# Scan decays by spread float32r products with an added mask, and a replanned attention, in a hybrid SSD / attention / PEER layer on one Trainium2 core

## The chip, the cores and the metric

The kernel runs on one core of one Trainium2 chip, in one launch. The metric is the device time of an execution in microseconds (us); it holds the span that the profile shows, from the first to the last instruction, and a little around it. The engines are PE (matrix products), DVE (vector), ACT (scalar functions), POOL and SP. SP, ACT and POOL also issue transfers (DMA). Each engine takes its instructions in program order, and an instruction that waits holds up what stands behind it on its engine.

## The reference

One layer (DEPTH = 1) on 512 latent and 256 context tokens of width 1024: a norm, one projection, three parallel mixers (a bidirectional Mamba-2 scan, pooling, neighbourhood attention), one output projection with a gated residual, a second norm, and a PEER feed-forward with 16384 experts. The scan is where the change is largest. Per chunk of 128 tokens, head and direction it computes

```
a_cs   = jnp.cumsum(a, axis=-1)                      # a = dt * a_head, per token and head
lmat   = jnp.exp(segsum(a))                          # exp(cs[l] - cs[s]) for s <= l, else 0
cb     = jnp.einsum('bclhn,bcshn->bhcls', cc, bc)    # one 128x128 matrix per chunk and group of 8 heads
y_diag = jnp.einsum('bhcls,bcshp->bclhp', cb * lmat, xd)   # xd = x * dt
y_off  = jnp.einsum('bclhn,bchpn->bclhp', cc, states[:, :-1]) * in_decay
```

once forward and once on the flipped sequence; the two results are added, gated by silu(z) and normed.

## The kernel before

The program runs through stages that the profile shows one behind the other: input projection and convolution (to about 203 us), the decays of the scan and the projection of V for the context (to 220), the scan (220 to 389), attention (to 486), the output projection and second norm (to about 560), and the PEER stage, which fills the rest of the span. Each projection product is written as three float32r products (high x high, low x high, high x low) with helper lines L186 to L188; a weight block arrives as `wraw`, ACT writes its float32r part `wh` (L176) and DVE (or POOL) the remainder `wl` (L179).

**The scan.** Its work is laid on steps by hand: `at(step, f, ...)` puts a piece on a step, and `run(step)` issues the pieces, each step together with six products of the projections of z, V and q. There are 16 *units* (4 chunks x 4 units of 4 heads), one every two steps, apart from two steps at the change of a chunk. A unit (c, u) consists of

- `u_in`: DVE writes `ms0` and `ms1` (mask times a, 128x512 each), and ACT writes eight 128x128 tiles, cb masked by a triangle and scaled by dt, into `t1` (forward) and `t2` (backward)
- `u_mm`, a step later: two float32 products of 128x512 that sum both directions' log decays into one PSUM tile `mm`
- `u_exp`, a step later: ACT takes one Exp over 128x512 into `ee`, DVE adds `t1` and `t2`
- `u_mul`, a step later: DVE multiplies by `ee`
- `u_diag`, a step later: PE's four products `yd` (float32, 128x64) with x.

Per chunk there are `c_mm` (cb of both groups, into an `mm` tile) and `c_mask` (four DVE products with a triangle). `st_in`, `st_mm`, `st_add` carry the states (`xd`, `mm<-xd,Bn`, `sfw` and `SB`), `o_mm`/`o_add` the part from the states. All of `u_mm`, `c_mm`, `st_mm`, `o_mm` share two PSUM buffers `mm`; `psT` (tile `pt`) has one buffer, `psY` holds `yd`. `f_load` to `f_store` gate, norm and transpose the result.

**Around it.** `decays` (L703) makes six Exps from sums of `an` (= a) by constant triangles. `q_out` scales q out of PSUM into `qT`. In the attention, `items` lists the weight blocks and mixer results that are split, and `OI` the steps at which that is issued; `o_first` starts the output projection with the pool part (`mBh`, `mBl`), and `o_part` goes on with it between the attention's own products (`sps`, `pt`, `po`). After it, `h_square` and `norm2` make the second norm of four token tiles, `norm2_split` its float32r parts `u2h` and `u2l`, and `q_part` and the first `u_block`s are the first products that use them.

## Time and profile before

| what | value |
| --- | --- |
| median of 3 runs | 1778.91 us (1778.72 to 1785.7) |
| profiled execution, its own time | 1779.43 us |
| its span, first to last instruction | 1777.6 us |
| TensorE clock granted, mean | 0.999 |
| PE busy | 1750.7 us (98%) |
| DVE, ACT, POOL busy | 1396.9, 837.6, 354.3 us |

The profile's page gives busy times by engine, the chain of work that ended last, and the costliest groups of instructions. Its trace can be asked for stretches of time, for groups by line and shape, for what an engine waited on, and for single instructions. In such rows L with a number is the line of the kernel before, a tile's buffer number is left out, and `<-ACT ee L895` behind an idle time names the instruction whose end released it. Matmul records overlap, since the engine is pipelined, so the distance from start to start is what a product takes in a row of products.

### The profile page before, as it was taken

The page shows a single profiled execution, that of the slowest core. Times are in us where ns is not written, and L with a number is a line of the kernel's source. Part 1 is how long each engine was busy: PE and PEld are TensorE (multiplying, and loading weights), DVE is VectorE, ACT ScalarE, POOL GpSimd, SP SyncE. Part 2 cuts the span into 40 slices and gives each one's busy share as a digit, 9 for nine tenths or more (in the row PEclk, how much of TensorE's full clock was granted, in tenths as well). Part 3 has the DMA queues.
Part 4 walks back from the last instruction along what each step waited for, and adds up shares of the span by engine and source line. Part 5 has one row for each costly group of instructions (what it writes and reads, how often), then busy time and mean ns, then how long its engine had stood idle before and what let it go on. Part 6 is the DMA issues. An engine that isn't in the chain of part 4 may idle for free.

```text
span 1777.6 us, 26116 instructions
## 1 busy us (share of the span) xinstructions
PE 1750.7 (98%) x9583; PEld 1503.8 (85%) x9583; DVE 1396.9 (79%) x2648; ACT 837.6 (47%) x1495; POOL 354.3 (20%) x248
## 2 busy tenths in 40 slices
PE   7999999999999999999999999999999999999998
PEld 6888776677788889999999998888888888888886
DVE  5689477976536589889999978878878888888876
...
GB/s 361 124 154 226 166 83 67 70 241 234 96 135 160 126 116 112 187 252 253 335 354 333 345 315 399 403 353 342 360 341 352 328 401 365 346 348 342 367 251 82
DMA packets 191905, 454.38 MB, mean 256 GB/s; under 512 B 13817, under 2 KB 117497, under 8 KB 173825
## 3 DMA queue, kind: packets, MB, share of 16 engines
...
q14 instruction: 54, 0.43, 0.1%
HBM read 400.09 MB, written 54.67 MB: 256 GB/s over the span
## 4 chain that ended last, share of the span: by engine, by line
PE 91%; DMA 3%; DVE 3%; ACT 2%; issue 1%; SPq 0%; POOL 0%; ACTq 0%; DVEq 0%; POOLq 0%
PE pv L188 10%; PE pv L186 10%; PE pv L187 10%; PE pu L186 9%; PE pu L188 9%; PE pu L187 9%; PE acc L186 5%; PE acc L188 5%; PE acc L187 5%; PE mm L889 2%; PE acc L406 1%; PE acc L411 1%; PE acc L408 1%; PE gdps L1695 1%; PE gdps L1696 1%; PE sps L1091 1%
## 5 line engine op out<-in xcount | busy, mean ns | idle before, releaser
L179 DVE TENSOR_TENSOR wl<-wraw,wh 128x1024 fp32r<-128x1024 f32 x294 | 367.3, 1262 | 101.5 <-ACT wh L176 99.1
L176 ACT ACTIVATE wh<-wraw 128x1024 fp32r<-128x1024 f32 x328 | 341.0, 1052 | 206.1 <-PE acc L187 76.7
L186 PE MATMUL pu<-u2h,wh 128*128 128x384 f32 x1024 | 349.7, 342 | 0.0
L188 PE MATMUL pu<-u2h,wl 128*128 128x384 f32 x1024 | 345.5, 337 | 0.4 <-DVE wl L179 0.4
L187 PE MATMUL pu<-u2l,wh 128*128 128x384 f32 x1024 | 344.8, 337 | 0.8 <-DVE u2l L179 0.8
L1634 POOL DMA_INDIRECT row<-in_peer_uv,idxG x128 | 156.6, 1223 | 807.9 <-DVE accG L1648 713.9
L186 PE MATMUL pv<-wh,wwh 128*128 128x512 f32 x768 | 301.2, 392 | 0.6 <-ACT wh L176 0.6
L187 PE MATMUL pv<-wl,wwh 128*128 128x512 f32 x768 | 300.5, 391 | 0.8 <-DVE wl L179 0.8
L188 PE MATMUL pv<-wh,wwl 128*128 128x512 f32 x768 | 300.9, 392 | 0.0
L187 PEld LDWEIGHTS pu<-u2l,wh 128*128 128x128 f32 x1024 | 192.5, 188 | 2.9 <-DVE u2l L179 1.1
L186 PEld LDWEIGHTS pu<-u2h,wh 128*128 128x128 f32 x1024 | 192.3, 188 | 1.8
L188 PEld LDWEIGHTS pu<-u2h,wl 128*128 128x128 f32 x1024 | 192.2, 188 | 1.3 <-DVE wl L179 1.3
L188 PEld LDWEIGHTS pv<-wh,wwl 128*128 128x128 f32 x768 | 144.2, 188 | 32.2
L187 PEld LDWEIGHTS pv<-wl,wwh 128*128 128x128 f32 x768 | 144.2, 188 | 31.9 <-DVE wl L179 1.8
L186 PEld LDWEIGHTS pv<-wh,wwh 128*128 128x128 f32 x768 | 144.2, 188 | 30.7 <-ACT wh L176 1.0
L1648 DVE SCALAR_TENSOR_TENSOR accG<-row,wG,accG 128x1024 f32<-128x1024 f32 x127 | 162.5, 1279 | 4.6 <-ACT wG L1643 3.3
L1639 DVE CUSTOM_DVE_ANT_0 row<-row,u2G 128x1024 f32<-128x1024 f32 x128 | 155.2, 1219 | 0.0
L176 ACT ACTIVATE wwh<-acl 128x384 fp32r<-128x384 f32 x86 | 45.2, 526 | 205.7 <-DVE acl L1807 139.7
L1698 ACT ACTIVATE stg<-gdps 128x512 f32<-128x512 f32 x96 | 101.4, 1169 | 19.4 <-PE gdps L1696 12.9
L179 POOL TENSOR_TENSOR wl<-wraw,wh 128x1024 fp32r<-128x1024 f32 x34 | 81.7, 2406 | 108.4 <-ACT wh L176 76.9
L1801 ACT ACTIVATE act<-pu 128x384 f32<-128x384 f32 x42 | 20.6, 491 | 159.3 <-PE pu L188 159.3
L1807 DVE TENSOR_TENSOR act<-act,gd 128x384 f32<-128x384 f32 x42 | 23.4, 558 | 84.4 <-ACT act L1801 84.4
...
## 6 DMA issues: line engine op xcount, KB each, us to landing
wraw<-in_peer_ut SPq DMA_DIRECT2D x128, 512.0 KB, 8.4
wraw<-in_peer_uv SPq DMA_DIRECT2D x128, 512.0 KB, 9.1
...
```

Source lines behind the costliest of these rows:

```text
L176: S.activation(hi, full, AF.Copy)
L179: (eng or V).tensor_tensor(lo, full, hi.bitcast(F32), ALU.subtract)
L186: PE.matmul(ps, ah, bh, start=start, stop=False)
L187: PE.matmul(ps, ah, bl, start=False, stop=False)
L188: PE.matmul(ps, al, bh, start=False, stop=stop)
L889: PE.matmul(ps, m, ms[d].rearrange("p a b -> p (a b)"), start=d == 0, stop=d == 1)
L1634: G.indirect_dma_start(out=rows[k], out_offset=None, in_=A["peer_uv"], in_offset=bass.IndirectOffsetOnAxis(ap=idxG[:, k:k + 1], axis=0))
L1639: V.tensor_tensor_reduce(row[:, 0:D], row[:, 0:D], u2G, 1.0, 0.0, ALU.mult, ALU.add, actG[:, k:k + 1])
L1648: V.scalar_tensor_tensor(accG, row[:, D:2 * D], wG[:, k:k + 1], accG, ALU.mult, ALU.add)
L1698: S.activation(stg[:, :, t0:t0 + 4].rearrange("p a t -> p t a"), ps, AF.Copy, scale=1.0 / GSCALE)
L1801: S.activation(ac[a], pu[:, :TD], AF.Gelu)
L1807: V.tensor_tensor(xq, xq, gds.pop(a), ALU.mult)
```

## The change

1. **Log decays.** Behind the pool projection PE makes the cumulative sums of `a` for all chunks and heads in both directions (`pcs`, 64 rows x 256). They are split into a float32r part and its remainder (`csT[0]` by ACT, `csT[1]` by DVE), written to DRAM (`cs_d`) and read back as 16 rows of a tile `rows` (128 x 2048) whose other 112 rows POOL sets to zero. `u_mm` becomes four float32r products: a column of `sel` spread over 128 columns picks the two rows (part and remainder) of a chunk and direction and puts their sum on all partitions; `idr` (identity) adds `neg0` or `neg1`, which hold -1e30 in the triangle that is to vanish. The forward direction goes into `pt` (psT), the backward one into `mm`.
2. **Exps.** `u_in` is gone. `u_exp` takes eight Exps of 128x128 with the negative cumulative sum (`ncs`) as bias per partition, and ACT scales two of the four backward tiles by dt; `u_mul` scales the other two on DVE (128x256), joins the directions with four `scalar_tensor_tensor` of 128x128, and multiplies by `cb`, which `c_copy` now only copies from PSUM. `u_diag` and `y_add` come a step later. The tiles of z that sat in `ms0`/`ms1` move into `SB`.
3. **Attention.** The last `q_out` is on DVE, `qT` is two tiles, block w0 is split earlier and w6 is split within the attention, the low part of pool block 4 is made by DVE rather than POOL, and its eight products stand at steps +5 and +6 rather than +2. The loads of `h` go from steps 12 to 15 to 36 to 45, that of `g1r` from 16 to 34.
4. **Second norm.** The mean square is put together by one DVE operation ahead of the square root rather than two around it; the norm of the third tile comes ahead of a split; the first q products and the first two PEER blocks take their late operand's products last (`mm_late`); the split of the first PEER block's low part goes from POOL to DVE.

```diff
+    ncs = [si.tile([P, NX, NH], F32, name=f"ncs{d}") for d in range(2)]
+    csT = [ad1.tile([NX * NH, 2, P], F32R, name=f"csT{i}") for i in range(2)]
+    pcs = psG.tile([P, 512], F32, name="acc")[0:NX * NH, 0:2 * P].rearrange("p (d t) -> p d t", d=2)
+    for d, m in enumerate((U_in, L_in)):
+        tc.keep_in_program_order(PE.matmul(pcs[:, d, :], an[:, d, 0:NX, :].rearrange("p t h -> p (t h)"), m, start=True, stop=True))
+    S.activation(csT[0], pcs, AF.Copy)
+    V.tensor_tensor(csT[1], pcs, csT[0].bitcast(F32), ALU.subtract)
+    for i in range(2):
+        nc.scalar.dma_start(cs_d[i].rearrange("d p t -> p d t"), csT[i].bitcast(F32))
     decays([(SU, 0, enF), (SL, 1, enB), (ONE, 0, toF)])
...
+        if b == 3:
+            V.tensor_scalar(dst, acc, HD ** -0.5, None, ALU.mult)
+        else:
+            S.activation(dst, acc, AF.Copy, scale=HD ** -0.5)
...
+    rows = m1.tile([P, NH * P], F32R, name="rows")
+    G.memset(rows[0:112].bitcast(F32), 0.0)
+    nc.scalar.dma_start(rows[112:P].bitcast(F32), cs_d.rearrange("i d (c h) t -> (i d c) (h t)", c=NX))
+    sel = m1.tile([P, 8], F32R, name="sel")
+    V.tensor_tensor(sel, ident[:, 112:120], ident[:, 120:P], ALU.add)
+    idr = m1.tile([P, P], F32R, name="idr")
+    V.tensor_copy(idr, ident)
+    negs = []
+    for d, m in enumerate((SU, SL)):
+        negs.append(m1.tile([P, P], F32R, name=f"neg{d}"))
+        V.tensor_scalar(negs[d], m, -1e30, None, ALU.mult)
...
-            V.tensor_tensor(ms[d], mb(msk), hb(an[:, d, c, hs]), ALU.mult)
...
-        for d, (t, tri) in enumerate(((t1, "U"), (t2, "L"))):
-            for j in range(4):
-                S.activation(t[:, j, :], cbm[g, tri], AF.Copy, scale=dtn[:, d, c, u * 4 + j:u * 4 + j + 1])
...
+    def u_mm(c, u):
+        un[c, u] = []
+        for d in range(2):
+            ps = psM.tile([P, 512], F32, name="mm") if d else psT.tile([P, 4, P], F32, name="pt").rearrange("p a b -> p (a b)")
+            x = 4 * d + c
+            PE.matmul(ps, sel[:, x:x + 1].broadcast_to([P, P]), rows[:, u * 512:(u + 1) * 512], start=True, stop=False)
+            PE.matmul(ps, idr, mb(negs[d]), start=False, stop=True)
+            un[c, u].append(ps)
+
+    def u_exp(c, u):
+        pf, pb = un[c, u]
         t1 = m2.tile([P, 4, P], F32, name="t1", bufs=3)
         t2 = m2.tile([P, 4, P], F32, name="t2")
...
-        S.activation(ee.rearrange("p a b -> p (a b)"), ps, AF.Exp)
-        V.tensor_tensor(t1, t1, t2, ALU.add)
-        un[c, u] = [ee, t1]
+        for j in range(4):
+            h = u * 4 + j
+            S.activation(t1[:, j, :], pf[:, j * P:(j + 1) * P], AF.Exp, bias=ncs[0][:, c, h:h + 1])
+        for j in range(4):
+            h = u * 4 + j
+            S.activation(t2[:, j, :], pb[:, j * P:(j + 1) * P], AF.Exp, bias=ncs[1][:, c, h:h + 1])
+        for j in range(2):
+            S.activation(t2[:, j, :], t2[:, j, :], AF.Copy, scale=dtn[:, 1, c, u * 4 + j:u * 4 + j + 1])
...
-        V.tensor_tensor(t1, t1, ee, ALU.mult)
+        t1, t2 = un[c, u]
+        V.tensor_tensor(t2[:, 2:4, :], t2[:, 2:4, :], dtn[:, 1, c, u * 4 + 2:u * 4 + 4].unsqueeze(2).broadcast_to([P, 2, P]), ALU.mult)
+        for j in (2, 3, 0, 1):
+            V.scalar_tensor_tensor(t1[:, j, :], t1[:, j, :], dtn[:, 0, c, u * 4 + j:u * 4 + j + 1], t2[:, j, :], ALU.mult, ALU.add)
+        V.tensor_tensor(t1, t1, mb(cbm[u // 2, "r"]), ALU.mult)
...
-            at(b + 2 * u + 4, u_diag, c, u)
-            at(b + 2 * u, u_in, c, u)
+            at(b + 2 * u + 5, u_diag, c, u)
             at(b + 2 * u + 1, u_mm, c, u)
...
-    items = [("w", 4), ("p", 4), ("p", 5), ("w", 5), ("s", 0), ("s", 1), ("s", 2), ("s", 3), ("w", 0), ("w", 1), ("w", 2), ("w", 3)]
+    items = [("w", 4), ("p", 4), ("p", 5), ("w", 5), ("s", 0), ("w", 0), ("s", 1), ("s", 2), ("s", 3), ("w", 1), ("w", 2), ("w", 3), ("w", 6)]
...
-    OI = [0, 0, 3, 4, 8, 10, 13, 15, 16, 28, 41, 54]
+    OI = [0, 0, 3, 4, 8, 11, 14, 18, 21, 28, 41, 54, 58]
...
-    at(O0 + 2, o_first, True)
+    at(O0 + 5, o_first, True, (0, 1))
+    at(O0 + 6, o_first, True, (2, 3))
...
-        at(O0 + 12 + t, nc.scalar.dma_start, h[:, t, :], A["x"][t * P:(t + 1) * P, :])
+        at(O0 + 36 + 3 * t, nc.scalar.dma_start, h[:, t, :], A["x"][t * P:(t + 1) * P, :])
...
+    def mm_late(ps, us, c, w, ks, late, first, last):
+        n = len(ks)
+        terms = [(k, x) for k in ks for x in ([(0, 0), (1, 0)] if late == "w" else [(0, 0), (0, 1)])]
+        terms += [(k, (0, 1) if late == "w" else (1, 0)) for k in ks]
+        for i, (k, (a, b)) in enumerate(terms):
+            PE.matmul(ps, w[b][:, k, :], us[a][:, k, c], start=first and i == 0, stop=last and i == 3 * n - 1)
...
-    q_part(0, early, range(4))
+    mm_late(pqs[0][:, early], (u2h, u2l), early, wqs[0], range(4), "u", True, False)
...
-    e_split(AHEAD[0], 0, G)
+    e_split(AHEAD[0], 0, None, alows)
```

On PE, at the second unit of chunk 0, the order before (names are output <- moving or stationary operands; `acc` rows belong to the z projection):

```order
1013 L889 MATMUL mm<-ms_2133,cst 128x512
1014 L889 MATMUL mm<-ms_2135,cst 128x512
1015 L186 MATMUL acc<-wh,uh 128x512
1016 L187 MATMUL acc<-wl,uh 128x512
1017 L188 MATMUL acc<-wh,ul 128x512
1018 L186 MATMUL acc<-wh,uh 128x512
1019 L187 MATMUL acc<-wl,uh 128x512
1020 L188 MATMUL acc<-wh,ul 128x512
1021 L831 MATMUL mm<-xd,Bn 128x512
1022 L909 MATMUL yd<-xsn,t_2097 128x64 x4
```

and with the change, from the state's product behind the first unit to the end of the second unit:

```order
1025 L859 MATMUL mm<-xd,Bn 128x512
1026 L186 MATMUL acc<-wh,uh 128x512
1027 L187 MATMUL acc<-wl,uh 128x512
1028 L188 MATMUL acc<-wh,ul 128x512
1029 L186 MATMUL acc<-wh,uh 128x512
1030 L187 MATMUL acc<-wl,uh 128x512
1031 L188 MATMUL acc<-wh,ul 128x512
1032 L934 MATMUL yd<-xsn,t_2139 128x64 x4
1033 L902 MATMUL pt<-rows,sel 128x512
1034 L903 MATMUL pt<-neg_2041,idr 128x512
1035 L902 MATMUL mm<-rows,sel 128x512
1036 L903 MATMUL mm<-neg_2043,idr 128x512
```

Two float32 products have become four float32r ones; between two units there are still twelve `acc` products and one `mm<-xd`, and `yd` has moved from behind `mm<-xd` to a place directly ahead of the next unit's first product.

On ACT, the second and third unit of chunk 0 before:

```order
159 L895 ACTIVATE ee<-mm 128x512
160 L882 ACTIVATE t_2187<-cbU_2077,dtn 128x128 x4
161 L882 ACTIVATE t_2188<-cbL_2079,dtn 128x128 x4
162 L895 ACTIVATE ee<-mm 128x512
163 L882 ACTIVATE t_2230<-cbU_2077,dtn 128x128 x4
```

and the first two of the change:

```order
158 L912 ACTIVATE t_2139<-pt,ncs_1888 128x128 x4
159 L915 ACTIVATE t_2140<-mm,ncs_1889 128x128 x4
160 L917 ACTIVATE t_2140<-t_2140,dtn 128x128 x2
161 L176 ACTIVATE wh<-wraw 128x1024
162 L912 ACTIVATE t_2187<-pt,ncs_1888 128x128 x4
163 L915 ACTIVATE t_2188<-mm,ncs_1889 128x128 x4
164 L917 ACTIVATE t_2188<-t_2188,dtn 128x128 x2
```

The eight small operations were independent of `u_mm`; now they all come behind it and read its PSUM tiles, and two more follow. On DVE, by the diff, four operations of 128x512 in a unit have become one of 128x256, four of 128x128 and one of 128x512, all behind the Exps, and four of 128x128 per chunk have become one copy of 128x256.

On PE at the second pair of heads of the attention, where the low products of the pool part (`mBl`) stand, before:

```order
1449 L1225 MATMUL acc<-wl,mBh 128x512
1450 L1222 MATMUL acc<-wh,mBl 128x512 x8
1451 L1091 MATMUL sps<-kT,qT 128x256 x4
1452 L1121 MATMUL pt<-cst,pr 128x128 x8
1453 L186 MATMUL acc<-wh,mBh 128x512
```

and with the change:

```order
1481 L1250 MATMUL acc<-wl,mBh 128x512
1482 L1116 MATMUL sps<-kT,qT_95 128x256 x4
1483 L1146 MATMUL pt<-cst,pr 128x128 x4
1484 L1247 MATMUL acc<-wh,mBl 128x512 x4
1485 L1146 MATMUL pt<-cst,pr 128x128 x4
1486 L1247 MATMUL acc<-wh,mBl 128x512 x4
1487 L186 MATMUL acc<-wh,mBh 128x512
```

The eight products that stood ahead of the scores `sps` now stand four by four behind the two transposes `pt`, which share the one buffer of `pt`.

## Rows read from the trace of the kernel before

**Rows 1.** The profile's page: busy time and share of the span by engine, and the chain that ended last by engine.

```profile
PE 1750.7 (98%) x9583; PEld 1503.8 (85%) x9583; DVE 1396.9 (79%) x2648; ACT 837.6 (47%) x1495; POOL 354.3 (20%) x248
PE 91%; DMA 3%; DVE 3%; ACT 2%; issue 1%; SPq 0%; POOL 0%; ACTq 0%; DVEq 0%; POOLq 0%
```

**Rows 2.** Busy time of each engine in stretches of the span: length, then PE, PEld (weight loads), DVE, ACT, POOL with their instructions, granted clock, DMA share and GB/s.

```profile
250.00:300.00 50.00, 50.00 (x210) 34.77 (x208) 37.79 (x62) 24.82 (x65) 1.01 (x1) 1.00 0.24 69
300.00:348.00 48.00, 47.31 (x188) 31.19 (x188) 44.53 (x58) 23.33 (x62) 15.38 (x9) 1.00 0.20 61
389.00:486.00 97.00, 93.85 (x652) 67.49 (x654) 58.80 (x172) 57.98 (x127) 27.47 (x17) 1.00 0.54 177
```

**Rows 3.** The chain of waits from 203 to 389 us: start, length, what. The first is the decays' sums, then the first and the last of the 16 units' products.

```profile
207.09 1.31 PE acc L701 x12
232.41 1.72 PE mm L889 x4
346.09 1.72 PE mm L889 x4
```

**Rows 4.** PE's instructions in order of time around two units of the scan: start, time of the record, line, operation.

```profile
267.93 1.88 PE L889 MATMUL mm<-ms,cst 128*128 128x512 f32 x4
...
270.10 0.39 PE L188 MATMUL acc<-wh,ul 128*128 128x512 f32 x1
270.33 0.39 PE L186 MATMUL acc<-wh,uh 128*128 128x512 f32 x1
...
274.15 1.88 PE L889 MATMUL mm<-ms,cst 128*128 128x512 f32 x4
```

**Rows 5.** DVE's groups by line and shape from 220 to 389 us: busy time of the group, mean of one in ns, idle time before.

```profile
L877 DVE TENSOR_TENSOR ms<-cst,an 128x512 f32<-128x512 f32 x32 | 22.3, 737 | 0.0
L901 DVE TENSOR_TENSOR t<-t,ee 128x512 f32<-128x512 f32 x16 | 15.3, 957 | 0.0
L896 DVE TENSOR_TENSOR t<-t,t 128x512 f32<-128x512 f32 x16 | 13.1, 817 | 0.0
L869 DVE TENSOR_TENSOR cbU<-mm,cst 128x128 f32<-128x128 f32 x8 | 2.3, 284 | 1.0 <-PE mm L861 0.9
```

**Rows 6.** DVE's groups by line and shape over the whole span: operations of the shapes that the change adds, from other stages.

```profile
L179 DVE TENSOR_TENSOR ucl<-uf,uch 128x256 fp32r<-128x256 f32 x8 | 3.3, 418 | 0.0
L1342 DVE TENSOR_SCALAR uf<-pt,sc2T,sh2T 128x128 f32<-128x128 f32 x16 | 5.5, 405 | 3.3 <-PE pt L1332 3.2
L1591 DVE SCALAR_TENSOR_TENSOR j<-pf,a4i 128x128 f16<-128x128 f32 x4 | 1.1, 288 | 0.0
```

**Rows 7.** ACT's groups by line and shape from 203 to 389 us.

```profile
L882 ACT ACTIVATE t<-cbU,dtn 128x128 f32<-128x128 f32 x64 | 20.3, 391 | 4.5 <-DVE cbU L869 4.5
L895 ACT ACTIVATE ee<-mm 128x512 f32<-128x512 f32 x16 | 9.6, 598 | 47.5 <-PE mm L889 39.2 <-DVE t L901 5.9 <-DVE t L896 2.4
L703 ACT ACTIVATE inB<-acc 128x96 f32<-128x96 f32 x1 | 0.3, 295 | 0.0
```

**Rows 8.** ACT and its queue in order of time behind the pool projection.

```profile
207.85 0.33 ACTq L679 DMA_DIRECT2D mix_d<-pa  x1
...
211.22 1.06 ACT L176 ACTIVATE wh<-wraw 128x1024 fp32r<-128x1024 f32 x1 [0.76 <-PE acc L188]
```

**Rows 9.** DVE in order of time at the start of the scan, and PE's first state product, which uses the last of these.

```profile
220.09 0.16 DVE L535 SCALAR_TENSOR_TENSOR sc2T<-pt,colv 128x8 f32<-128x8 f32 x1
220.47 2.00 DVE L179 TENSOR_TENSOR wl<-wraw,wh 128x1024 fp32r<-128x1024 f32 x1 [0.22 <-ACT wh L176]
222.39 2.39 DVE L824 TENSOR_TENSOR xd<-xsn,enB 128x512 f32<-128x512 f32 x1
...
225.96 1.02 PE L831 MATMUL mm<-xd,Bn 128*128 128x512 f32 x2
```

**Rows 10.** PE's waits in order of time: the wait for an Exp in the scan, then those in the attention and the second norm; the time in brackets is how long PE stood idle.

```profile
314.20 1.12 PE L831 MATMUL mm<-xd,Bn 128*128 128x512 f32 x2 [0.69 <-ACT ee L895]
...
389.20 0.70 PE L1091 MATMUL sps<-kT,qT 64*128 64x256 f32 x4 [0.69 <-ACT qT L769]
...
398.56 0.63 PE L1121 MATMUL pt<-cst,pr 128*128 128x128 f32 x4 [0.78 <-ACT pT L1126]
...
416.38 0.63 PE L1121 MATMUL pt<-cst,pr 128*128 128x128 f32 x4 [1.05 <-ACT pT L1126]
...
452.14 1.13 PE L1091 MATMUL sps<-kT,qT 64*128 64x256 f32 x6 [0.75 <-ACT pr L1108]
...
543.77 0.36 PE L187 MATMUL acc<-u2l,wh 128*128 128x256 f32 x1 [0.43 <-DVE ssq L1322]
...
551.52 0.44 PE L187 MATMUL pu<-u2l,wh 128*128 128x384 f32 x1 [0.84 <-DVE u2l L179]
```

**Rows 11.** ACT, its queue and DVE in order of time at three of those waits: the copy of `pT` behind a transfer's issue, the last `qT` with the `wl` that DVE has at the time, and the pair of `u2l`.

```profile
415.20 0.33 ACTq L1032 DMA_DIRECT2D nb<-in_nabias  x1
415.63 0.60 ACT L1126 ACTIVATE pT<-pt 128x512 f32<-128x512 f32 x1 [1.12 <-PE po L1139]
...
388.55 0.60 ACT L769 ACTIVATE qT<-acc 128x512 f32<-128x512 f32 x1 [2.90 <-PE acc L188]
...
387.76 1.22 DVE L179 TENSOR_TENSOR wl<-wraw,wh 128x1024 fp32r<-128x1024 f32 x1
...
548.73 3.34 DVE L179 TENSOR_TENSOR u2l<-uf,u2h 128x512 fp32r<-128x512 f32 x2
```

More of the change, by code (lines that the diff above doesn't have):

```diff
@@ L269, in build @@
     kT = na1.tile([P, 4, NTOK], F32, name="kT")
-    qT = na1.tile([P, 4, SEQ], F32, name="qT")
+    qTs = [na1.tile([P, 2, SEQ], F32, name=f"qT{i}") for i in range(2)]
     vc = na1.tile([P, 2, 512], F32, name="vc")
@@ L305, in build @@
     xT = a1.tile([P, KB, NTOK], F32, name="xT")
-    kf, qf, vf = (ap.rearrange("p a b -> p (a b)") for ap in (kT, qT, vc))
-    xin = [kf[:, t * D:(t + 1) * D] for t in range(3)] + [qf[:, t * D:(t + 1) * D] for t in range(2)] + [vf]
+    kf, q0f, q1f, vf = (ap.rearrange("p a b -> p (a b)") for ap in (kT, *qTs, vc))
+    xin = [kf[:, t * D:(t + 1) * D] for t in range(3)] + [q0f, q1f, vf]
     for t in range(NT):
@@ L878, in u_in @@
+    def u_exp(c, u):
+        pf, pb = un[c, u]
         t1 = m2.tile([P, 4, P], F32, name="t1", bufs=3)
         t2 = m2.tile([P, 4, P], F32, name="t2")
-        for d, (t, tri) in enumerate(((t1, "U"), (t2, "L"))):
-            for j in range(4):
-                S.activation(t[:, j, :], cbm[g, tri], AF.Copy, scale=dtn[:, d, c, u * 4 + j:u * 4 + j + 1])
-        un[c, u] = [ms, t1, t2]
-    def u_mm(c, u):
-        ms, t1, t2 = un[c, u]
-        ps = psM.tile([P, 512], F32, name="mm")
-        for d, m in enumerate((SU, SL)):
-            PE.matmul(ps, m, ms[d].rearrange("p a b -> p (a b)"), start=d == 0, stop=d == 1)
-        un[c, u] = [ps, t1, t2]
@@ L1204, in build, with o_first @@
     O0 = A0
-    OI = [0, 0, 3, 4, 8, 10, 13, 15, 16, 28, 41, 54]
+    OI = [0, 0, 3, 4, 8, 11, 14, 18, 21, 28, 41, 54, 58]
     at(O0, i_load, 3)
     at(O0, i_load, 4)
-    before(O0, i_low, 1)
     before(O0, i_high, 1)
-    for i in range(2, 12):
+    at(O0 + 2, i_low, 1)
+    for i in range(2, len(items)):
         before(O0 + OI[i], i_high, i)
         at(O0 + OI[i], i_low, i)
-    at(O0 + 16, row_bc, g1r, 1, 0, nc.scalar)
-    def o_first(low):
-        for t in range(NX):
+    at(O0 + 34, row_bc, g1r, 1, 0, nc.scalar)
+    def o_first(low, ts):
+        for t in ts:
             ts_ = slice(t * P, (t + 1) * P)
@@ L1228, in o_part @@
         out_mm(accs[t], ispls[kk], kk, t, False, False)
[L1229 to L1230 removed]
+    at(O0 + 1, o_first, False, range(NX))
+    at(O0 + 5, o_first, True, (0, 1))
+    at(O0 + 6, o_first, True, (2, 3))
     for j, kk in enumerate((5, 0, 1, 2, 3)):
@@ L1278, in out_end @@
         S.activation(tmp, h[:, t, hs], AF.Square, accum_out=ssq[:, t, half:half + 1])
+        V.scalar_tensor_tensor(ssq[:, t, 0:1], ssq[:, t, 0:1], 1.0 / D, epsc, ALU.mult, ALU.add)
     for kk in (6, 7):
-        w = out_w(kk, 0)
+        w = ispls[6] if kk == 6 else out_w(kk, 0)
         for t in range(NX):
@@ L1428, in build @@
     ahead = ahead_steps(lambda: u_depth[0])
-    pus = [u_block(*sp[AHEAD[0], 0])]
-    norm2_T(3)
-    norm2_scale(3)
-    pus.append(u_block(*sp[AHEAD[1], 0]))
+    pus = []
+    for m in range(2):
+        pus.append(psu())
+        mm_late(pus[m][:, :TD], (u2h, u2l), slice(0, TD), sp[AHEAD[m], 0], range(KB), "w", True, True)
+        if m == 0:
+            norm2_T(3)
+            norm2_scale(3)
     norm2_split(3, 0)
```

65 lines of the change are left out of this document (34 added, 31 removed).

## The prediction, made before the change was run

> **What bounds the kernel now.** I read the page first, for the engine on which the chain lies: PE is busy 98% of the span and carries 91% of the chain, DVE and ACT 3% and 2% [rows 1]. Then the stretches, for what each stage waits on: from 250 to 300 us PE is busy all 50.00, from 300 to 348 it is 47.31 of 48.00 while DVE is busy 44.53 (93%) and ACT 23.33, and in the attention PE has 3.15 us idle of 97 [rows 2]. So inside the scan the price of an edit is the PE time that it takes away, as long as DVE and ACT keep up; in the attention it is the single waits of PE. The chain of waits gives the size of the scan's part: `u_mm` stands in it with 1.72 us for each of 16 units [rows 3]. The clock is at its upper level throughout (1.00 in each stretch of [rows 2]), so nothing is to be had from it.
>
> **Scan, PE.** Six projection products follow each other every 0.23 us (270.10, 270.33 in [rows 4]); they are float32r and 128x512, as the four new ones are. `u_mm` was two float32 products, four records, 1.72 us. Four times 0.23 is 0.92, so a unit saves 0.80 and the 16 units 12.8 us. That is the largest term, and PE is what the chain follows there, so I take it whole. The period of two steps was 274.15 − 267.93 = 6.22 us [rows 4] and becomes 5.42. The bounds: no PE time saved if a product with a spread operand takes 0.43 (half a float32 product, two records of 0.43 each), and 12.8 at the rate of the row. No row has a product whose stationary or moving operand is one column or one block spread by repetition; the nearest in type and size is that of [rows 4], and I take it.
>
> **Added PE work.** The cumulative sums are two float32 products of 64x128 outputs, four records; the decays' twelve records of 96 columns took 1.31 us [rows 3], so four take some 0.45.
>
> **Front of the scan.** ACT gets a copy of 64x256 and two transfer issues of 0.33 each [rows 8], with the wait for DVE's remainder between, some 1.5 us in all, ahead of the Exps of the decays; behind those the first `wh` waited 0.76 for PE [rows 8]. So 0 to 0.8 us can reach PE. DVE gets four small operations (`sel`, `idr`, `neg0`, `neg1`) behind `sc2T`; at 0.28 (cbU, [rows 5]) they take 1.1 us, of which 0.22 was idle time ahead of `wl`, and push `xd`, which ended at 224.78 and is used at 225.96 [rows 9]: 1.18 us of slack against 0.9, so nothing or a few tenths. `rows` is issued behind three `wh`, some 12 us ahead of the first `u_mm` at 232.41 [rows 3]; POOL's zeroing lies there too. I take +0.5 for the front, bounds 0 and 1.6.
>
> **Scan, DVE and ACT.** DVE's unit was two `ms` (22.3/32 each), the sum (13.1/16), the product (15.3/16), and a quarter of four triangle products of 0.28 [rows 5]: 1.39 + 0.82 + 0.96 + 0.28 = 3.45 us. It becomes 0.42 for 128x256 and four times 0.29 for 128x128 [rows 6], 0.70 for 128x512 (22.3/32, [rows 5]), 0.1 for the copy: 2.4. With the dearer 0.405 [rows 6], an operation with two operands per partition, it is 2.8. In 300 to 348 there are six units; DVE goes from 44.5 to some 38.3 us, while the stretch itself shrinks by 4.8 to 43.2: 89% rather than 93%. It is no looser by much, but no tighter. ACT's unit was eight small ones at 20.3/64 = 0.32 and one Exp of 0.60 [rows 7]: 3.1 us; ten small ones are 3.2 at the same price. Exps of 128x96 out of PSUM took 0.295 [rows 7], so 0.32 is a fair price for 128x128, and 0.39 (the mean of one, unoverlapped) the upper bound: 3.9. ACT then has 3.2 to 3.9 of a period of 5.42, with `wh` (1.06, [rows 8]) in about every other one.
>
> What is new is the wait. Before, ACT's small ones needed no `u_mm`; now all eight Exps stand between `u_mm` and the release of its two PSUM buffers. `pt` and the `mm` of the unit are wanted again a period later, 4.5 us after `u_mm` ends; eight Exps take 2.5 to 3.1. That holds in the steady part. Where `c_mm` or an `o_mm` or state product comes between, the buffer is wanted after one `xd` product (0.86, half of 1.72) and six of 0.23: 2.2 us. At some six such places PE could wait 0.3 to 0.9 us: 0 to 4, I take +1.2. At one of them it waited before, 0.69 for the single `ee` [rows 10], and that wait is replaced: −0.7. Net +0.5. `u_diag` comes one step later to make room for the longer ACT and DVE chain, 3.2 + 2.4 us and what queues there, of some 9 us from `u_mm` to `yd`; it needs no more.
>
> At this place a rule speaks against the change. The Trainium skill ("VectorE: DVE Perf Modes", section "The TRN2 errata — SBUF-src ops pay a fixed extra latency per instruction") has vector and scalar operations pay a fixed cost per instruction and advises tiles of at least 512 elements. Its table would give an Exp of 128 columns out of PSUM 300 cycles at 1.2 GHz, an estimate of 0.25 us, against 0.57 for one of 512, so eight cost 2.0 where one cost 0.57. The trace agrees that small ones are dear (0.32 for 128 columns, 0.60 for 512, [rows 7]); but the kernel before pays for eight of them already. What it would make of the time is the first rival.
>
> **Attention and tail.** `q_out` of the last block goes to DVE, which is then in a `wl` from 387.76 to 388.98 [rows 11]; its 128x512 (0.70, as `ms` in [rows 5]) would end at about 389.7 where ACT's ended at 389.15. PE waits for it (0.69 at 389.20, [rows 10]); that grows by 0.5, bounds 0 and 0.9. The wait of 0.78 at 398.56 is the second `pt` for the copy of the first out of the one buffer; four products of 0.23 now stand between and cover it. The wait of 1.05 at 416.38 is a `pT` that ACT began at 415.63, held by the issue of `nb` at 415.20 [rows 11] behind loads of `h`, which now come 24 steps later: gone too. The wait of 0.75 at 452.14 stays, its two weight splits stand together as before. Together −1.8; bounds −3 (all 3.15 idle us of [rows 2]) and +2, should a moved split come late. In the second norm PE waits 0.43 for a `u2l` and 0.84 for the next [rows 10]; late operands last covers the first with eight products, and the second is shortened since the pair of `u2l` took 3.34 us [rows 11] in place of two times 0.7 beside POOL's split, which is moved to DVE behind them: −1.0, bounds −1.3 and +1.
>
> **Sum.** −12.8 + 0.45 + 0.5 + 0.5 + 0.5 − 1.8 − 1.0 = −13.65. The profiled execution took 1779.43, its span 1777.6 and 1.83 around it; 1779.43 − 13.65 = 1765.8. The median of the runs, 1778.91, lies 0.5 lower, so I forecast 1765.3. The PEER stage is untouched and only starts earlier. A measurement of this kernel can hardly tell less than 0.5%, 8.9 us, from no change.
>
> **Rivals.** (1) ACT becomes the gate, by the rule above. If a small Exp costs 0.39 and does not overlap, ten are 3.9, and with `wh` or a z copy every period is full; a unit then loses some 0.5 us to `pt` or `mm`, 8 us in all: 1773, within 0.5%. For it: the Exps are in order behind `wh`, which itself waits for PE. Against: ACT is busy half the time from 250 to 348 [rows 2], and 20.3/64 is with overlap. 0.12. (2) The spread products don't run at the float32r rate. At the float32 price of 0.86 each, `u_mm` takes 3.44 us, 1.72 more, 27.5 us over 16 units: 1779 + 27.5 − 1 = 1805. It decides from 0.43 per product on, where nothing is saved. No row speaks for it. 0.04. (3) The replanned attention goes wrong: the splits moved to DVE there make `mBl` or `qT` late at several places, 3 to 6 us more than forecast: 1768 to 1771, on either side of the 1770.0 from which it counts as faster. 0.10. (4) The waits cost nothing and the attention loses all its idle time: −12.8 + 0.45 − 0.7 − 3 − 1.3, 1762. 0.12.
>
> **Chances.** The forecast with its own bounds, 1762 to 1769, has 0.62. Faster by over 0.5% holds the forecast, (4), and a good half of (3): 0.80. Within 0.5% holds (1) and the rest of (3): 0.16. Slower: (2), 0.04. The range goes from 1759.5, a little beyond (4) since its bounds add up, to 1772.5, past (3) and just short of (1), and leaves out about 0.16.
>
> **What would show it.** `u_mm` should stand as four records 0.23 apart, and two units 5.4 us apart; PE should be busy as fully as before from 250 to 348, with DVE just under 90%. PE waits on ACT's `t` ahead of `c_mm` or `mm<-xd` would be the new wait; if they stand at every unit, rival 1 is right. The scan should end about 12 us earlier, and the first `sps` of the attention wait about a microsecond for DVE. The forecast is wrong if a new product's start to start is well over 0.23, or if DVE runs solid.

## The result, and the profile after

The changed kernel takes 1767.76 us (median of 6 runs, 1765.78 to 1770.83) against 1779.93 us of the kernel before (median of 6); the ratio is 0.9937, 95% interval 0.9926 to 0.9947, so 9 to 13 us faster. A second set of runs gave 1767.12 against 1778.91, ratio 0.9936 (0.9919 to 0.9953). The forecast was 1765.3 with 1759.5 to 1772.5. The profiled execution took 1769.83 us, its span is 1768.1.

The page after, busy time and chain, which answer to [rows 1]:

```profile
PE 1740.0 (98%) x9587; PEld 1505.5 (85%) x9587; DVE 1388.4 (79%) x2678; ACT 835.1 (47%) x1511; POOL 348.6 (20%) x247
PE 93%; DVE 4%; ACT 1%; DMA 1%; issue 1%; ACTq 0%; POOL 0%; DVEq 0%; SPq 0%
```

PE lost 10.7 us of work and is still the chain. The stretches, as in [rows 2] (the second and third moved by the time already won):

```profile
250.00:300.00 50.00, 50.00 (x234) 38.56 (x233) 41.25 (x81) 30.38 (x92) 0.00 (x0) 1.00 0.30 90
300.00:345.00 45.00, 44.11 (x191) 31.39 (x190) 40.86 (x69) 22.49 (x63) 17.69 (x11) 1.00 0.25 74
378.00:475.00 97.00, 94.32 (x664) 68.08 (x664) 61.89 (x177) 57.99 (x126) 25.82 (x16) 1.00 0.58 178
```

PE is about as full in the scan as before (44.11 of 45.00, 47.31 of 48.00 before), and DVE is 91% busy from 300 to 345 (40.86 of 45.00). Two units of the scan on PE, the answer to [rows 4]:

```profile
270.45 0.48 PE L902 MATMUL pt<-rows,sel 128*128 128x512 f32 x1
270.77 0.40 PE L903 MATMUL pt<-neg,idr 128*128 128x512 f32 x1
271.00 0.40 PE L902 MATMUL mm<-rows,sel 128*128 128x512 f32 x1
271.24 0.40 PE L903 MATMUL mm<-neg,idr 128*128 128x512 f32 x1
...
275.90 0.48 PE L902 MATMUL pt<-rows,sel 128*128 128x512 f32 x1
```

The spread products start 0.23 us apart, as the projections do, and the period is 5.45 us. Only the first of a unit, now directly behind `yd`, takes 0.32.

To see where time went I compare the start of the same product in both traces. The last q product ends the scan, the last `mBl` product the attention and the output projection, the 129th `pu` lies behind the second norm, and `pu` and `pv` are the products of the PEER stage with its first and its second weights. How much earlier than in the kernel before a product starts (us, negative is later):

| kernel | first z product | last q product | first score | last `mBl` product | 129th `pu` | first `pv` | end of span | PE idle for one weight block |
| --- | --- | --- | --- | --- | --- | --- | --- | --- |
| before | 0 | 0 | 0 | 0 | 0 | 0 | 0 | 0.56 + 0.76 |
| the change | -1.1 | 10.4 | 10.0 | 12.3 | 11.7 | 11.7 | 9.6 | 2.08 + 0.76 |
| the change again | -0.6 | 11.0 | 10.5 | 12.9 | 12.5 | 12.5 | 13.9 | 0.35 |
| scan only | -1.3 | 10.4 | 10.4 | 9.3 | 9.3 | 9.3 | 7.3 | 1.76 + 0.77 |
| attention only | -0.5 | -0.6 | -1.1 | 1.3 | 2.1 | 2.2 | 4.1 | 0.11 |
| old norm | -0.4 | 11.2 | 10.7 | 11.2 | 11.1 | 11.1 | 12.7 | 0.27 |
| tail order | -1.5 | 10.1 | 9.6 | 12.0 | 11.9 | 11.9 | 13.5 | 0.22 |
| u twice | -1.3 | -2.6 | -3.1 | -0.7 | -1.2 | -1.2 | 0.4 | 0.19 |
| u in float32 | -0.2 | -26.5 | -27.0 | -24.6 | -25.1 | -25.1 | -24.2 | 0.76 |
| ACT more | -0.7 | 8.4 | 8.0 | 8.6 | 9.4 | 9.4 | 10.9 | 0.34 |
| tail order 2 | -1.1 | 10.2 | 9.7 | 12.1 | 13.8 | 13.9 | 13.3 | 1.26 + 0.76 |
| tail order 2, q on ACT | -1.1 | 10.5 | 10.5 | 12.8 | 14.4 | 14.4 | 10.4 | 3.26 + 0.46 |

In the first profile of the change the lead at the first `pv` product (1051.58 us) is 11.7 us, and only 9.6 at the end: 1.9 are gone within 20 us behind it, at one wait and the lower clock that followed it. The second profile of the same kernel has 12.5 and gains 1.4 instead. The last column tells the two apart.

### The profile page after: what moved, and what is told of

It reads as the page before. It is cut to its first block, busy times and chain, and to the rows that moved or that the text cites. A ratio compares the mean times of both kernels' runs of the same rounds, so it can differ in the third digit from the quotient of the medians.

```text
span 1768.1 us, 26186 instructions
## 1 busy us (share of the span) xinstructions
PE 1740.0 (98%) x9587; PEld 1505.5 (85%) x9587; DVE 1388.4 (79%) x2678; ACT 835.1 (47%) x1511; POOL 348.6 (20%) x247
## 3 DMA queue, kind: packets, MB, share of 16 engines
q8 instruction: 75, 1.23, 0.3%
## 4 chain that ended last, share of the span: by engine, by line
PE 93%; DVE 4%; ACT 1%; DMA 1%; issue 1%; ACTq 0%; POOL 0%; DVEq 0%; SPq 0%
PE pu L186 10%; PE pu L188 10%; PE pu L187 10%; PE pv L188 10%; PE pv L186 10%; PE pv L187 10%; PE acc L186 5%; PE acc L187 5%; PE acc L188 5%; PE acc L407 1%; PE acc L412 1%; PE acc L409 1%; PE gdps L1738 1%; PE gdps L1739 1%; PE sps L1116 1%; PE pt L1146 1%
## 5 line engine op out<-in xcount | busy, mean ns | idle before, releaser
L179 DVE TENSOR_TENSOR wl<-wraw,wh 128x1024 fp32r<-128x1024 f32 x295 | 361.9, 1239 | 93.3 <-ACT wh L176 91.8
L186 PE MATMUL pu<-u2h,wh 128*128 128x384 f32 x1008 | 344.3, 342 | 0.0
L188 PE MATMUL pu<-u2h,wl 128*128 128x384 f32 x1008 | 340.0, 337 | 0.0
L187 PE MATMUL pu<-u2l,wh 128*128 128x384 f32 x1008 | 339.3, 337 | 0.0
## 6 DMA issues: line engine op xcount, KB each, us to landing
wraw<-in_peer_uv SPq DMA_DIRECT2D x128, 512.0 KB, 10.1
gd<-gd_d SPq DMA_DIRECT2D x15, 1536.0 KB, 12.1
```

Source lines behind the costliest of these rows:

```text
L179: (eng or V).tensor_tensor(lo, full, hi.bitcast(F32), ALU.subtract)
L186: PE.matmul(ps, ah, bh, start=start, stop=False)
L187: PE.matmul(ps, ah, bl, start=False, stop=False)
L188: PE.matmul(ps, al, bh, start=False, stop=stop)
```

## The experiments

My theory after the result: the scan gives what PE no longer computes; the attention gives its waits; the second norm gives nothing; and something in the PEER stage takes some back. The rivals: the gain is DVE's relief rather than PE's time; ACT is close to being the gate; the PEER stage gives back because PE arrives earlier than its transfers.

**The scan part alone.** The edit is parts 1 and 2 of the change on the kernel before.

> The kernel before with the scan part of the change alone (cumulative sums, spread float32r products, small Exps, c_copy), attention and second norm as before. Theory, by the trace of the changed kernel: the front costs 0.8 us, the scan gives 11.6, the attention and the norm keep their waits; PE is 10.8 us earlier at the first score product than before, and a transfer-bound stretch of the PEER stage near 1070 us gives 1 to 2 us of it back: 9 to 10 us under the kernel before. Rival, that the replanned attention carries a good part of the gain: 7 us or less.

Measured: 1772.49 us, ratio 0.9957 (0.9943 to 0.9972), 6.3 us under the kernel before where I had expected 9 to 10: by the time alone that is the rival's bound of 7 or less. The table says where the rest went: the last q product is 10.4 us earlier, as in the whole change, but the old attention then loses 1.1 of it, and 2.0 are gone behind the first `pv`. Its waits, to be held against those of [rows 10] at 398.56 and 416.38 us:

```profile
388.91 0.63 PE L1142 MATMUL pt<-cst,pr 128*128 128x128 f32 x4 [1.50 <-ACT pT L1147]
...
407.22 0.50 PE L187 MATMUL acc<-wl,mAh 128*128 128x512 f32 x1 [0.84 <-DVE wl L179]
...
412.73 0.52 PE L1142 MATMUL pt<-cst,pr 128*128 128x128 f32 x3 [0.79 <-ACT pT L1147]
```

The first has doubled from 0.78 to 1.50: ACT's copy of `pT` stands behind a `wh` that waits for a block of `w_out`, and that block does not come earlier by as much as the scan ends earlier. So the earlier scan alone makes the old attention worse.

**The attention and norm alone.** Parts 3 and 4 on the kernel before.

> The kernel before with the attention and second norm of the change alone. Theory: the last scaling of q on DVE costs 0.5 us, the attention's waits give 2.4 back, the second norm costs 0.6: 1.3 us under the kernel before when the PEER stage begins, and as little lead, so the transfer-bound stretch near 1070 us takes nothing: 1 to 1.5 us faster. Rival, that the two parts help each other (a wait of the attention is only gone with the faster scan): no change.

Measured: 1775.68 us, ratio 0.9983 (0.9973 to 0.9993). By the table -1.1 at the first score, +1.3 at the end of the output projection, so the attention gives 2.4; the second norm gives another 0.8, where I had expected a loss of 0.6. With that, and only 0.11 us idle for the weight block, the time is 3.1 us under the kernel before rather than 1.0 to 1.5. The two parts add up, 9.3 + 2.2 = 11.5 at the first `pv` against 11.7 and 12.5 of the whole change, but by luck: behind the faster scan the new attention is worth 1.1 more (the old one loses that), and the new norm 1.2 to 1.5 less.

**The old second norm in the changed kernel.** Part 4 undone; its core:

```diff
-        S.activation(std2[:, t:t + 1], ssq[:, t, 1:2], AF.Sqrt, bias=ssq[:, t, 0:1], scale=1.0 / D)
...
-        V.reciprocal(ssq[:, t, 1:2], std2[:, t:t + 1])
-        V.tensor_scalar(xns[t], h[:, t, :], ssq[:, t, 1:2], None, ALU.mult)
+        V.tensor_tensor(ssq[:, t, 0:1], ssq[:, t, 0:1], ssq[:, t, 1:2], ALU.add)
+        r = rstd_of(o2, ssq[:, t, 0:1], 1, D)
+        V.tensor_scalar(xns[t], h[:, t, :], r, None, ALU.mult)
...
-    e_split(AHEAD[0], 0, None, alows)
+    e_split(AHEAD[0], 0, G)
```

> The changed kernel with the second norm and the first PEER products as before (scan and attention changed). Theory: what the new order saves at one wait it loses at the next, since the pair of low splits meets another split of POOL: PE is 0.4 to 0.9 us earlier at the end of the q products than in the changed kernel, total the same within 1 us. Rival, as forecast: the new order gives 1.0 us, so this kernel is 1.0 us slower.

Measured: 1766.75 us, ratio 0.9929 (0.9916 to 0.9942): no difference that can be measured. Between the last `mBl` product and the 129th `pu` it loses 0.03 against the kernel before, where the change loses 0.6. But it is not 0.6 ahead there, since its attention lost 1.9 us to the clock: it gains 0.5 from the first score to the last `mBl` product, the change 2.4. Stretches of this kernel and then of the change, granted clock in the third column from the end:

```profile
438.00:442.00 4.00, 2.93 (x15) 1.78 (x16) 3.68 (x10) 1.97 (x5) 1.03 (x1) 0.88 0.63 196
442.00:448.00 6.00, 6.00 (x38) 4.72 (x38) 1.84 (x7) 2.83 (x7) 2.02 (x2) 0.79 0.82 272
```

```profile
438.00:442.00 4.00, 2.93 (x18) 1.83 (x16) 3.93 (x10) 2.42 (x6) 0.31 (x1) 1.00 0.56 179
442.00:448.00 6.00, 6.00 (x46) 4.44 (x44) 2.50 (x10) 2.81 (x7) 2.82 (x2) 1.00 0.97 304
```

The same two waits of 0.75 and 0.32 us stand in both (439 to 442 us, the pair of weight splits that the change leaves together). In one execution the clock then falls to its lower level for some microseconds, in the other it doesn't. The run with more on ACT, below, lost 1.8 us there in the same way.

**The tail order.** Two edits in the second norm:

```diff
+                if t == 3:
+                    norm2_split(t - 2, 0)
                 h_square(t - 1)
...
-                    e_split(*pieces[m], u_eng[0] if m < n else V, lows if m > i else None)
+                    e_split(*pieces[m], u_eng[0] if 2 < m < n else V, lows if m > i else None)
```

> The changed kernel with two edits in the second norm: for the last early tile the high split of u2 stands ahead of the square of the next tile on ACT, and the low split of the third PEER block is made by DVE, not POOL. Theory: the 0.77 us that PE waits for that high split and the 1.09 us that it waits for the last pair of low splits (which take 3.5 us beside POOL's split, against 1.3 alone) both go: 1.5 to 1.9 us faster when the PEER stage begins, 1 to 2 us in all. Rival, that the waits move on to the norm of the third tile or to the weights: under 0.5 us.

Measured: 1766.10 us, ratio 0.9924 (0.9912 to 0.9937), from which no gain on the change is shown. The first edit works: the wait of 0.77 is gone, and `pu` begins 12.9 us ahead of the kernel before rather than 12.1. The second missed its aim. The split that runs on POOL at that time is that of a q weight block and not the one I moved, so the last pair of `u2l` took 3.49 us as before, and waits of 0.34 and 1.10 stand at it: half of the theory missed.

**The spread products twice.** Every unit's four products issued twice.

```diff
+            for _ in range(2):
+                PE.matmul(ps, sel[:, x:x + 1].broadcast_to([P, P]), rows[:, u * 512:(u + 1) * 512], start=True, stop=False)
+                PE.matmul(ps, idr, mb(negs[d]), start=False, stop=True)
```

> The changed kernel with the four spread products of each unit issued twice into the same PSUM tiles (the second time overwrites the first). Theory, that PE's time is the price in the scan: four products of 0.23 more per unit, 0.92 x 16 = 14.7 us later at the first score product than the changed kernel, a little less where PE waited for DVE before (0.8 us at one place): 13 to 15. Rival, that DVE (91% busy there) or ACT sets the pace: under 8.

Measured: 1779.04 us, ratio 1.000 (0.999 to 1.001); 13.1 us later at the first score product than the change (-3.1 against 10.0). PE's time is the price. Most of the difference to 14.7 is waits for DVE that vanish (1.23 us in the scan of the change, 0.14 here), since PE is now full:

```profile
300.00:345.00 45.00, 45.00 (x198) 33.53 (x197) 36.47 (x66) 21.18 (x66) 13.22 (x8) 1.00 0.25 76
```

**The spread products in float32.** `rows`, `sel`, `idr` and `neg` as float32.

```diff
-    rows = m1.tile([P, NH * P], F32R, name="rows")
+    rows = m1.tile([P, NH * P], F32, name="rows")
...
-    sel = m1.tile([P, 8], F32R, name="sel")
+    sel = m1.tile([P, 8], F32, name="sel")
```

> The changed kernel with rows, sel, idr and neg in float32, so that the same four products run as float32; everything on ACT and DVE stays as in the change. Theory: a product takes 0.86 rather than 0.23 us, 2.5 us more per unit, 40 us in all: about 1807, 28 above the kernel before. That is what the second rival of the prediction would have cost. Rival, that the gain of the change comes from DVE's or ACT's relief: within 10 us of the changed kernel.

Measured: 1803.37 us, ratio 1.0136 (1.0117 to 1.0154); 37.0 us later at the first score product than the change. With DVE and ACT left as in the change and PE's products dear, the whole gain is gone and more: what DVE and ACT do in the change gives nothing where PE's products are dear. Rival 2 of the prediction was priced about right (1805), and did not occur.

**More on ACT.** Four more copies of 128x128 in each unit.

```diff
+        for j in range(4):
+            S.activation(t1[:, j, :], t1[:, j, :], AF.Copy)
```

> The changed kernel with four more ACT copies of 128x128 per unit (each forward tile onto itself), behind the others. Theory, that ACT has room: 1.2 to 1.3 us more on ACT per unit of a period of 5.4, 20 us in all, and under 2 us at the first score product. The first rival of the prediction, that ACT is the gate: 8 us or more.

Measured: 1768.06 us, ratio 0.9936 (0.9920 to 0.9951), no difference to the change; 2.0 us later at the first score product, a little more than I allowed, of which the later start took none (it began 0.4 earlier). ACT's busy time in two stretches of the scan goes from 30.38 and 22.49 to

```profile
250.00:300.00 50.00, 49.10 (x228) 37.22 (x227) 39.81 (x79) 33.76 (x112) 0.00 (x0) 1.00 0.29 90
300.00:345.00 45.00, 43.87 (x191) 31.28 (x190) 40.66 (x69) 27.14 (x91) 16.48 (x10) 1.00 0.22 67
```

and PE has 2 us of waits there, all for DVE, which gets the tiles later. The total doesn't show it, since its second norm gained 0.9 us and PE stood only 0.34 us for the weight block of the PEER stage. Some 15 us of ACT's time (the copies are busy 15.2 us in all, not the 20 I had expected) cost 2.4: ACT is not the gate, but the chain ACT to DVE to PE has little room left.

**The tail order once more.** The first edit as above, and the split that in truth runs on POOL at that time moved to DVE.

```diff
-            wqs[hi + 1] = wspl(wq[hi + 1], KB, G if hi > 1 else V)
+            wqs[hi + 1] = wspl(wq[hi + 1], KB, G if hi > 2 else V)
```

> The changed kernel with the high split ahead of the square as in the run of the tail order before, and with the low split of the fourth q weight block on DVE, where it stands ahead of the pair of low splits, instead of on POOL beside it. Theory, that the pair is slow because POOL runs a split at the same time: the pair takes 1.3 to 1.5 us rather than 3.5, the waits of 0.34 and 1.10 go, and PE is 1.3 to 1.5 us earlier at the later products than with the first tail order, 1764 to 1765 in all. Rival, that the pair is slow for its own sake: no difference.

Measured: 1766.07 us, ratio 0.9922 (0.9908 to 0.9935). The pair in the change, POOL's split beside it and PE's wait for it, and then the pair in this kernel:

```profile
546.88 3.48 DVE L179 TENSOR_TENSOR u2l<-uf,u2h 128x512 fp32r<-128x512 f32 x2 [2.01 <-ACT u2h L176]
...
547.15 2.67 POOL L179 TENSOR_TENSOR wl<-wraw,wh 128x1024 fp32r<-128x1024 f32 x1
...
550.42 0.39 PE L187 MATMUL acc<-u2l,wh 128*128 128x256 f32 x1 [1.09 <-DVE u2l L179]
```

```profile
546.11 1.29 DVE L179 TENSOR_TENSOR u2l<-uf,u2h 128x512 fp32r<-128x512 f32 x2
```

In the trace the theory holds: 1.29 us without POOL's split, no wait, and 13.8 us ahead at the 129th `pu` against 11.7. In the times it isn't shown: 1766.07 us where I had expected 1764 to 1765, against 1766.10 for the first tail order; 2.02 us went to the weight block of the PEER stage. The Trainium skill has the rule for the pair ("SBUF — State Buffer", section "Who interferes with whom"): DVE and POOL share a pair of ports, a DVE instruction with two SBUF inputs contends for it with a POOL instruction that reads SBUF, and the one that holds it blocks the other for its whole instruction. The trace agrees: the pair takes 2.2 us longer beside a POOL split of 2.67.

**The change again**, for a second profile, and **the second tail order with the last q on ACT** in one set of runs. The edit of the latter to the second tail order:

```diff
-        if b == 3:
-            V.tensor_scalar(dst, acc, HD ** -0.5, None, ALU.mult)
-        else:
-            S.activation(dst, acc, AF.Copy, scale=HD ** -0.5)
+        S.activation(dst, acc, AF.Copy, scale=HD ** -0.5)
```

> The changed kernel itself once more, for another profiled execution. Theory, that the wait of the PEER stage for a weight block near 1070 us (2.1 us in its first profile, up to 0.3 in six of the other kernels, whatever their lead) belongs to the execution and not to the change: up to the end of the gathered projections the trace is the same within 0.3 us as in the first profile, and the block lands anywhere from 15 to 18 us behind the first product of that part, so the span lies between 1764 and 1768. Rival, that the change's own timing sets it: the block lands 17.9 us behind again, and the span is 1768.

> The kernel of the second tail order with the last scaling of q back on ACT. Theory: DVE held that scaling behind a low split, so PE waits 0.69 rather than 1.17 us ahead of the first score product, 0.5 us less; the high split of the pool block that ACT then makes later comes 0.6 us later and is covered by the score products. Total 0.5 us under the kernel of the second tail order, within what can be measured. Rival, that the later split on ACT costs PE as much at the first products of the pool part: no change.

Measured: 1767.12 us (ratio 0.9936, 0.9919 to 0.9953) and 1765.22 us (0.9922, 0.9905 to 0.9938). For the change again the first part of the theory missed: the two traces are 0.8 us apart at the first `pv`, not 0.3. The second part holds: the span is 1763.7, just under the stated bound, and the block was there 15.1 us behind the first `pv` product, against 17.9 in the first profile. The weight block of the PEER stage, as ACT and PE wait for it, in the first profile of the change:

```profile
1069.43 1.06 ACT L176 ACTIVATE wh<-wraw 128x1024 fp32r<-128x1024 f32 x1 [5.96 <-DMA wraw<-in_peer_uv]
...
1070.54 0.50 PE L186 MATMUL pv<-wh,wwh 128*128 128x512 f32 x1 [2.08 <-ACT wh L176]
1071.80 0.80 PE L187 MATMUL pv<-wl,wwh 128*128 128x512 f32 x1 [0.76 <-DVE wl L179]
1072.39 0.63 PE L188 MATMUL pv<-wh,wwl 128*128 128x512 f32 x1
1072.82 0.63 PE L186 MATMUL pv<-wh,wwh 128*128 128x512 f32 x1
```

with its stretch behind the wait (busy times of the engines, then granted clock, share of the DMA engines and GB/s):

```profile
1070.00:1080.00 10.00, 8.70 (x31) 6.92 (x32) 8.45 (x11) 5.19 (x11) 2.04 (x2) 0.83 1.03 412
```

in the second one:

```profile
1065.87 1.06 ACT L176 ACTIVATE wh<-wraw 128x1024 fp32r<-128x1024 f32 x1 [3.18 <-DMA wraw<-in_peer_uv]
...
1068.24 0.50 PE L187 MATMUL pv<-wl,wwh 128*128 128x512 f32 x1 [0.35 <-DVE wl L179]
```

and the same stretch of it:

```profile
1070.00:1080.00 10.00, 9.92 (x47) 8.16 (x46) 8.97 (x13) 5.38 (x9) 1.70 (x2) 1.00 1.03 413
```

and in the kernel before:

```profile
1081.30 0.50 PE L186 MATMUL pv<-wh,wwh 128*128 128x512 f32 x1 [0.56 <-ACT wh L176]
1082.56 0.50 PE L187 MATMUL pv<-wl,wwh 128*128 128x512 f32 x1 [0.76 <-DVE wl L179]
```

The same kernel waits 2.84 us in one execution and 0.35 in another. Behind the long wait products start 0.43 us apart (1072.39, 1072.82) rather than 0.23, and the granted clock of that stretch is 0.83. Over all twelve profiles the idle time doesn't follow the lead: it is 0.11 at a lead of 2.2, 0.22 at 11.9, 3.72 at 14.4, and 1.32 at none. So the lead doesn't explain the wait, and what is left is a transfer whose landing varies, in a stretch where the DMA engines are full (share 1.03). Whether it varies by execution or by chip these two profiles can't tell, since they come from two sets of runs; within one set on one chip the other kernel's times go from 1764.12 to 1769.08. What sets the landing stays open.

The other kernel shows the price of the last q on DVE, its first score product

```profile
378.70 1.13 PE L1113 MATMUL sps<-kT,qT 64*128 64x256 f32 x8 [0.69 <-ACT qT L784]
```

against 1.17 us of idle time in the change:

```profile
379.25 1.10 PE L1116 MATMUL sps<-kT,qT 64*128 64x256 f32 x7 [1.17 <-issue]
```

and nothing lost behind it: 12.8 at the last `mBl` product against 12.1 in the second tail order. At the first `pv` product it leads by 14.4 us, 2.6 and 1.9 us more than the two profiles of the change. In the times, 1765.2 to 1767.1 in one set of runs, the intervals of the ratios overlap (0.9905 to 0.9938 against 0.9919 to 0.9953), so it is likely the better kernel and not shown to be.

## Why the prediction was right, and where not

**Scan, PE: the rate right, the sum 0.7 us too large.** The products run at 0.23, which was the open price; the two-fold and the float32 run confirm it from both sides. From the first z to the last q product the change gains 11.6 us (1.1 + 10.4) where the sum had 12.8 - 0.5. By the period (6.22 us before, 5.45 after) a unit saves 0.77 rather than 0.80, 0.5 of the 0.7. What the working missed is a cost of order: the first spread product stands behind `yd`, and its record is 453 ns against 397 of the others,

```profile
L902 PE MATMUL pt<-rows,sel 128*128 128x512 f32 x16 | 7.2, 453 | 0.0
L902 PE MATMUL mm<-rows,sel 128*128 128x512 f32 x16 | 6.4, 397 | 0.0
```

16 times 0.056, 0.9 us, of which some is won back where `yd` left.

**New waits in the scan: the size right (+0.5), the cause wrong.** PE's waits in the scan were 0.69 and 0.12 us before and are 0.08, 0.81 and 0.34 now, 0.4 more. I had PE wait for the Exps ahead of `c_mm` and of state products. The longest new wait does stand at a state product, but there PE waits for DVE's `ytmp`, which frees a buffer `mm`, since DVE's 128x256 product stands in its way beside a POOL operation:

```profile
319.96 1.50 DVE L922 TENSOR_TENSOR t<-t,dtn 128x256 f32<-128x256 f32 x1
321.50 1.14 DVE L924 SCALAR_TENSOR_TENSOR t<-t,dtn,t 128x128 f32<-128x128 f32 x4
...
323.28 0.69 DVE L950 TENSOR_TENSOR ytmp<-mm,inB 128x512 f32<-128x512 f32 x1
...
319.53 1.65 POOL L951 TENSOR_TENSOR y<-y,ytmp 128x512 f32<-128x512 f32 x1 [1.89 <-DVE ytmp L950]
...
324.02 1.13 PE L859 MATMUL mm<-xd,Bn 128*128 128x512 f32 x2 [0.81 <-DVE ytmp L950]
```

The chain is read from below: PE stands 0.81 us for `ytmp`, which is behind `t<-t,dtn`, 1.50 us long from 319.96 on, while POOL's 319.53 runs. In the groups this product has a mean of 0.69 us where I took 0.42: twelve of the sixteen took 0.42, and the four that began behind a POOL product took 1.50. The small ones took 0.37 where I had 0.29 or at most 0.405:

```profile
L924 DVE SCALAR_TENSOR_TENSOR t<-t,dtn,t 128x128 f32<-128x128 f32 x64 | 19.8, 371 | 0.6
L922 DVE TENSOR_TENSOR t<-t,dtn 128x256 f32<-128x256 f32 x16 | 11.1, 691 | 0.0
L912 ACT ACTIVATE t<-pt,ncs 128x128 f32<-128x128 f32 x64 | 18.3, 369 | 42.2 <-PE pt L903 42.2
L915 ACT ACTIVATE t<-mm,ncs 128x128 f32<-128x128 f32 x64 | 18.6, 398 | 0.0
L917 ACT ACTIVATE t<-t,dtn 128x128 f32<-128x128 f32 x32 | 11.8, 448 | 0.0
```

DVE's unit took 2.7 us, near the upper figure of 2.8, and its share 91% where I had 89%. ACT's took 3.0 us ((18.3 + 18.6 + 11.8) / 16), 3.2 forecast. So rival 1 did not occur, and the run with more on ACT shows that ACT was not the gate even with some 1 us more per unit. Small operations are dear, as that rival had it (0.37 to 0.45 us each for 128 columns), but ACT had the time for them.

**Front and sums: +0.95 forecast.** The first z product is 1.1 and 0.6 us later in the two profiles of the change; at the product ahead of the sums the first was already 0.35 later than the kernel before and the second 0.15 earlier, so the sums and the front cost 0.8 in both. DVE's four small operations took 3.5 us and not 1.1, but the split and `xd` behind them took 1.21 and 0.68 rather than the 2.00 and 2.39 of [rows 9], and PE's first state product waited for nothing.

**Last q on DVE: +0.5 forecast, 0.48 measured** (1.17 against 0.69 of [rows 10]).

**Attention: -1.8 forecast, -2.4 measured,** in all profiles with the new attention at full clock. Both waits named are gone, and that of 0.75 stayed, as said; a new one of 0.34 came:

```profile
412.22 1.13 PE L1116 MATMUL sps<-kT,qT 64*128 64x256 f32 x6 [0.34 <-ACT pr L1133]
...
440.15 1.13 PE L1116 MATMUL sps<-kT,qT 64*128 64x256 f32 x6 [0.75 <-ACT pr L1133]
441.60 0.63 PE L1146 MATMUL pt<-cst,pr 128*128 128x128 f32 x4 [0.32 <-DVE sm L1138]
```

PE's idle time from the first score to the last `mBl` product went from 3.09 to 1.52 us, so the waits give 1.6 of the 2.4. In the other 0.8 products start closer together in the new order; no run takes that apart, and the forecast had no such term. What I did not see either is that the old attention would have grown worse behind a faster scan (1.1 us in the run of the scan alone), so the replan is worth 3.5 there.

**Second norm: -1.0 forecast, +0.6 and +0.4 measured. This step failed.** The wait of 0.43 for `u2l` was replaced by one of 0.77 for `u2h`,

```profile
531.47 0.39 PE L1416 MATMUL acc<-u2h,wh 128*128 128x256 f32 x1 [0.77 <-ACT u2h L176]
```

because ACT makes it behind the square of the next tile and now the root as well; in the tail order, with the split ahead of them, that wait is gone. The wait of 0.84 went as forecast: the pair of `u2l` at which it stood took 1.45 us rather than the 3.34 of [rows 11]. But the pair of the last tile, 1.86 us long before, now met POOL's next split and took 3.48, and a new wait of 1.09 stands behind it. The pair of the third tile in the change, and that of the last tile in the kernel before:

```profile
535.92 1.45 DVE L179 TENSOR_TENSOR u2l<-uf,u2h 128x512 fp32r<-128x512 f32 x2
...
558.88 1.86 DVE L179 TENSOR_TENSOR u2l<-uf,u2h 128x512 fp32r<-128x512 f32 x2 [0.79 <-ACT u2h L176]
```

As the traces read, it hangs on ACT whether the last pair meets that split: ACT makes `u2h` behind a split of a q weight block, for which it waits. In the change, and then in the attention-only run with its pair and POOL's split:

```profile
543.72 1.06 ACT L176 ACTIVATE wh<-wraw 128x1024 fp32r<-128x1024 f32 x1 [5.00 <-DMA wraw<-in_peer_wq]
...
553.89 1.06 ACT L176 ACTIVATE wh<-wraw 128x1024 fp32r<-128x1024 f32 x1 [4.08 <-DMA wraw<-in_peer_wq]
...
557.04 1.29 DVE L179 TENSOR_TENSOR u2l<-uf,u2h 128x512 fp32r<-128x512 f32 x2 [1.09 <-ACT u2h L176]
...
558.23 2.41 POOL L179 TENSOR_TENSOR wl<-wraw,wh 128x1024 fp32r<-128x1024 f32 x1
```

In five profiles POOL's split began 0.15 to 0.56 us behind the pair, and the pair took 3.48 to 3.50; in the attention-only run and that with more on ACT it began 1.19 and 1.37 behind, the pair took 1.29, and the norm gained 0.8 and 0.9. So of the two waits that it named the forecast moved one to another operand and took one away, and it had no term for the next: with one split moved away from one pair, the next pair met the next split, or not, by when ACT came to it.

**The PEER stage "only starts earlier": too simple.** It contains waits for one weight block of 0.1 to 3.7 us over the twelve profiles, 2.84 and 0.35 in two executions of the same kernel, so it moves one run by more than several of the terms above. The sum for PE up to there, 11.7 and 12.5 us, is the fair comparison with the 13.65 forecast. The second norm alone is 1.6 and 1.4 short and the scan 0.7; the attention, with 0.6 more than forecast, covers a part. That the total came within 2.5 us of the forecast is so in part the luck of misses with opposite signs; the largest term, the scan on PE, is not.
